# Moving seven weight conversions of an eight-core decoder block to earlier steps

## The chip, the cores and the metric

The kernel runs on all 8 cores of one Trainium2 chip. Each core works on two of the 16 sequences; the cores do not exchange data. The metric is the device time of the slowest core, in microseconds (us), and fast executions are compared with fast executions. A program on all cores has a second, slower state in which the cores of one die, rarely of both, get a lower clock (one run of after took 2790 us, with a mean clock of 0.861 on one die and 0.997 on the other).

For effects of a few us I also use a quieter number, called the **core mean** here: the mean span of the four cores of a die, averaged over all dies of a kernel's timed runs whose four cores all had a granted clock above 0.99. It keeps the undisturbed die of a slow run and does not hang on the one slowest core. Its scatter from die to die is about 2 us; 8 to 21 dies stand behind each value for an experiment and its reference, so the difference of two core means is uncertain by about 0.5 to 1 us (1.6 for the noisiest kernel).

## The reference, cut to what matters

```python
def swiglu(h, w_gate, w_up, w_down):
    return (jax.nn.silu(h @ w_gate) * (h @ w_up)) @ w_down

x = x + 0.5 * swiglu(rmsnorm(x, ffn1_norm), ffn1_w_gate, ffn1_w_up, ffn1_w_down)   # FFN 1
h = rmsnorm(x, mix_norm) @ w_in                    # pool values | q | k | v | forget logits
...                                                # pooling mixer | forgetting attention, 8 heads
x = x + concat([y_pool, y_attn]) @ w_out
x = x + 0.5 * swiglu(rmsnorm(x, ffn2_norm), ffn2_w_gate, ffn2_w_up, ffn2_w_down)   # FFN 2
```

All weights are float32 inputs. x is 16 x 2048 x 1024; the FFN width is 2816, which is 22 blocks of 128.

## The kernel before

**Units and conversions.** The FFN work of a core is cut into eight units of 1024 tokens; a unit has 22 gate/up steps and 8 down steps (steps 22 to 29). Unit 3 is the first that uses FFN 2. Its gate and up weights are converted once from float32 to bf16, from DRAM to DRAM, by 22 DMAs issued from POOL (the GpSimd engine); each is released when the FFN reaches a given step of a given unit. Weights are then loaded through small rings: ring A (gate/up, three buffers), ring B (down, four halves) and ring M (mixer, two buffers). Attention and the mixer are interleaved with the FFN.

```python
UNITS = [(0, 0), (0, 1), (0, 2), (1, 0), (0, 3), (1, 1), (1, 2), (1, 3)]   # (FFN, group of tokens)
# ...
def converts():
    # ...
    jobs += [(2 + i // 18, i % 18, wgu[1][i], wgu_s[1][i], [("wgu", 1, i)]) for i in range(NFF)]
    jobs += [(3, 5 + 2 * i, wd[1][i], wd_s[1][i], both(1, i)) for i in range(NKC)]
    for n, (u, fl, src, dst, keys) in enumerate(jobs):
        tr.add_dma_sem(f"cv{n}")
        yield ev_step[(u, fl)]                      # wait until the FFN reaches step fl of unit u
        yield Op("pool", [], keys, lambda e, src=src, dst=dst: e.dma_start(out=dst, in_=src),
                 c_dma(128 * src.shape[-1] * 4), sem=f"cv{n}")
```

**A scheduler in the host program.** Streams (FFN, attention, loads, conversions, ...) yield operations with modelled costs. At build time the scheduler takes, again and again, the operation that its model says can begin first. So the order of instructions on every engine is fixed at build time, and it depends on the modelled time of every DMA, at an assumed rate of `DMA_GB = 285.0`.

```python
def emit(self, op):
    # ...
    if op.sem is not None:                                          # a DMA
        self.tr.dma(op.eng, op.sem, op.reads, op.writes, op.emit)
        self.free[op.eng] = t + (1000.0 if op.eng == "pool" else 60.0)
        other = self.dma_free["sp" if op.eng == "pool" else "pool"]
        begin = max(self.dma_free[op.eng], t + 1300.0)
        end = begin + op.cost                                       # later DMAs queue up behind it
        # ...
```

## Time and profile before

| | before |
|---|---|
| median of 40 runs | 2447.49 us (2444.03 to 2881.26; those over about 2481 are slow-state runs) |
| cores of the profiled run | 2437.7 to 2445.4 us, clock 0.996 to 0.998 |
| busy on the slowest core | TensorE 98%, VectorE 67%, ScalarE 59%, POOL 23% |

The page of the slowest core: the span, engine busy times with their shares, and the start of the chain of work that ended last, by engine.

```profile
span 2445.4 us, 39669 instructions; the slowest of 8 cores (2437.7 to 2445.4 us)
...
PE 2386.1 (98%) x11862; PEld 1074.2 (44%) x12094; DVE 1638.8 (67%) x2424; ACT 1440.4 (59%) x2857; POOL 569.7 (23%) x793
...
PE 87%; DMA 5%; ACT 3%; issue 3%; DVE 2%; SPq 0%; ACTq 0%; DVEq 0%; POOLq 0%; POOL 0%
```

TensorE is the bound. The Trainium skill, "Perfetto Trace Analysis", section "Identifying the Most-Contended Engine", warns that matmul busy share does not measure the distance to peak, because pipelined matmuls look smaller in a trace. So I use the 98% only to say where to look for lost time: in TensorE's idle gaps and in the stretches at a lower clock. Core 1 serves for the readings below. The timeline at the start of unit 2 (start and duration of the issue, engine, line, what is moved):

```profile
587.72 0.54 POOL L525 DMA_DIRECT2D wgu2s<-wgu  x1
...
588.31 3.00 SPq L576 DMA_DIRECT2D sb_xsF<-yT  x3
...
589.66 1.08 POOL L525 DMA_DIRECT2D wgu2s<-wgu  x2
...
592.93 0.54 SPq L576 DMA_DIRECT2D sb_xsF<-yT  x1
```

and the summary of those four loads of the mixer's input (`xsF`) in 585 to 612 us:

```profile
DMA to landing us min/median/max: 15.0/22.3/33.2
```

Three conversions and four 512 KB loads are issued within about 5 us, and the last load takes 33.2 us to land; the median of such loads over the whole run is 8.5 us on this core (8.0 on the slowest core's page). The windows of core 1 (stretch, busy time and count of each engine, granted clock, DMA share, GB/s):

```profile
core 1: us, PE busy (x) PEld busy (x) DVE busy (x) ACT busy (x) POOL busy (x), PEclk, DMA share, GB/s
540.00:590.00 50.00, 50.00 (x240) 22.29 (x238) 20.01 (x27) 2.69 (x8) 8.92 (x16) 1.00 0.83 261
590.00:640.00 50.00, 47.69 (x245) 19.37 (x244) 43.12 (x57) 43.05 (x95) 19.80 (x25) 0.97 0.90 181
...
1160.00:1180.00 20.00, 20.00 (x134) 11.57 (x132) 17.95 (x35) 6.30 (x16) 3.20 (x7) 1.00 0.75 237
```

TensorE is full at the end of unit 1 (540 to 590), loses 2.3 us at the start of unit 2, and the mean clock of 0.97 there is one stretch of 3.4 us at half clock, near 617. TensorE's waits on core 1 from 500 to 1200 us (who waited for whom: total us, times, longest):

```profile
PE ps L847 <- DMA sb_wA<-wgu1s: 2.3, 1, 2.3
PE ps L847 <- DVE sb_sg L305: 1.9, 3, 0.8
PE ps L1075 <- ACT sb_PT L1179: 1.3, 3, 0.7
...
PE ps L874 <- DVE sb_sg L305: 0.7, 1, 0.7
```

Line 847 is the gate/up matmul, 874 the down matmul, 897 the mixer's projections.

### The profile page before, as it was taken

How to read it: one execution, taken by the hardware profiler on the slowest of the kernel's cores; microseconds unless marked ns; L12 is line 12 of the kernel's file. 1: busy time of each engine (PE TensorE's matmuls, PEld its weight loads, DVE VectorE, ACT ScalarE, POOL GpSimd, SP SyncE). 2: the span in 40 equal slices, each digit the busy share in tenths (PEclk: the TensorE clock that was granted, in tenths of full speed). 3: DMA queues.
4: the chain of work that ended last, by engine and by line, in shares of the span. 5: the costliest groups of instructions: out<-in, count | busy, mean ns of one | idle time of the engine just before them, and what ended most of it. 6: DMA issues, size and time to landing. Idle time of an engine off the chain costs nothing.

```text
span 2445.4 us, 39669 instructions; the slowest of 8 cores (2437.7 to 2445.4 us)
## 1 busy us (share of the span) xinstructions
PE 2386.1 (98%) x11862; PEld 1074.2 (44%) x12094; DVE 1638.8 (67%) x2424; ACT 1440.4 (59%) x2857; POOL 569.7 (23%) x793
## 2 busy tenths in 40 slices
PE   8999999999899999999999999999999999999998
PEld 4444444444444444443445444453434434444444
DVE  5763658656886977598756687268696799634541
ACT  4652457743686747688535875169674799514540
POOL 0114213332331332213332113223133101110000
PEclk9999999999999999999999999999999999999999
DMA  7999777588747456763564334642544621463225
GB/s 180 189 215 223 174 192 160 122 222 217 184 131 190 154 163 168 194 164 89 186 209 168 120 122 131 209 134 84 194 139 149 198 94 61 140 207 112 77 75 151
DMA packets 126530, 384.61 MB, mean 157 GB/s; under 512 B 15088, under 2 KB 15216, under 8 KB 126320
## 3 DMA queue, kind: packets, MB, share of 16 engines
q0 software_dynamic: 57200, 215.25, 35.7%
q1 hardware_dynamic: 69120, 166.81, 20.6%
q8 instruction: 102, 1.67, 0.3%
q14 instruction: 108, 0.88, 0.1%
HBM read 362.73 MB, written 91.24 MB: 186 GB/s over the span
## 4 chain that ended last, share of the span: by engine, by line
PE 87%; DMA 5%; ACT 3%; issue 3%; DVE 2%; SPq 0%; ACTq 0%; DVEq 0%; POOLq 0%; POOL 0%
PE ps L847 42%; PE ps L874 25%; PE ps L897 11%; PE ps L1075 3%; PE ps L1331 2%; PE ps L1116 2%; ACT sb_PT L1179 2%; DMA sb_wA<-wgu 1%; DMA sb_xsF<-yT 1%; PE ps L588 1%; DMA sb_wM<-wins 1%; PE ps L912 1%; PE ps L1159 0%; DMA sb_xsF<-xT 0%; DMA wgu1s<-sb_wA 0%
## 5 line engine op out<-in xcount | busy, mean ns | idle before, releaser
L847 PE MATMUL ps<-sb_hF,sb_wA 128*128 128x512 bf16 x5501 | 1254.4, 380 | 26.6 <-DVE sb_sg L305 6.1
L847 PEld LDWEIGHTS ps<-sb_hF,sb_wA 128*128 128x128 bf16 x5632 | 538.7, 98 | 698.8 <-issue 79.2
L874 PE MATMUL ps<-sb_act,sb_wB 128*128 128x512 bf16 x2753 | 623.0, 379 | 6.9 <-issue 2.5
L1179 ACT ACTIVATE sb_PT<-ps,sb_BT 128x256 bf16<-128x256 f32 (+1 forms) x1152 | 433.5, 491 | 118.3 <-PE ps L1075 59.7
L770 ACT ACTIVATE sb_sg<-sb_sg 128x512 f32<-128x512 f32 x352 | 227.5, 646 | 416.8 <-DVE sb_sg L767 395.2
L874 PEld LDWEIGHTS ps<-sb_act,sb_wB 128*128 128x128 bf16 x2816 | 272.0, 98 | 338.7 <-issue 18.7
L767 DVE TENSOR_TENSOR sb_sg<-sb_sg,ps 128x512 f32<-128x512 f32 x352 | 240.6, 684 | 159.1 <-PE ps L847 149.5
L783 DVE TENSOR_TENSOR sb_act<-sb_sg 128x512 bf16<-128x512 f32 x352 | 275.2, 782 | 70.3 <-ACT sb_sg L775 67.5
L1206 DVE TENSOR_TENSOR sb_acc<-sb_acc,sb_PT 128x1024 f32<-128x1024 f32 (+3 forms) x264 | 298.6, 1131 | 23.4 <-ACT sb_PT L1179 11.5
L772 ACT ACTIVATE sb_sg<-sb_sg,sb_cst 128x512 f32<-128x512 f32 x352 | 259.6, 737 | 20.6 <-ACT sb_sg L770 1.5
L815 DVE SCALAR_TENSOR_TENSOR sb_xr<-ps,sb_xr 128x512 f32<-128x512 f32 x128 | 88.0, 688 | 254.2 <-PE ps L874 237.3
L775 ACT ACTIVATE sb_sg<-sb_sg 128x512 f32<-128x512 f32 x352 | 227.2, 645 | 19.7 <-ACT sb_sg L772 0.7
L305 DVE COPY sb_sg<-ps 128x512 f32<-128x512 f32 x224 | 153.1, 683 | 47.2 <-PE ps L847 46.9
L897 PE MATMUL ps<-sb_hm,sb_wM 128*128 128x512 bf16 x755 | 176.7, 379 | 4.9 <-DMA sb_wM<-wins 4.0
L613 POOL TENSOR_TENSOR sb_na<-sb_na,sb_sq 128x512 f32<-128x512 f32 x120 | 149.6, 1247 | 66.0 <-ACT sb_sq L582 60.1
L582 ACT ACTIVATE sb_sq<-sb_xsF 128x512 bf16<-128x512 f32 x184 | 116.4, 655 | 66.4 <-DMA sb_xsF<-xT 27.1
L455 POOL DMA_DIRECT2D sb_wA<-wgu2s x88 | 47.9, 545 | 400.8 <-PE ps L847 327.9
L553 ACT ACTIVATE sb_rs<-ps,sb_cst 128x512 f32<-128x512 f32 x104 | 71.4, 691 | 86.4 <-PE ps L588 79.8
L897 PE MATMUL ps<-sb_yc,sb_wM 128*128 128x512 bf16 x499 | 119.8, 379 | 0.9 <-DVE sb_yc L1407 0.2
L1187 POOL TENSOR_SCALAR_AFFINE_SELECT sb_PT<-sb_PT 128x256 bf16<-128x256 bf16 x128 | 77.0, 605 | 176.1 <-ACT sb_PT L1179 175.4
L897 PEld LDWEIGHTS ps<-sb_hm,sb_wM 128*128 128x128 bf16 x768 | 74.7, 98 | 94.7 <-issue 6.3
L1271 DVE TENSOR_TENSOR sb_xsF<-ps,sb_xsF 128x512 f32<-128x512 f32 x64 | 44.2, 691 | 75.7 <-PE ps L897 75.7
(104 smaller groups left out, 1703.3 us busy)
## 6 DMA issues: line engine op xcount, KB each, us to landing
sb_xsF<-yT SPq DMA_DIRECT2D x96, 512.0 KB, 8.0
sb_wA<-wgu2s POOLq DMA_DIRECT2D x88, 512.0 KB, 3.8
sb_wA<-wgu1s POOLq DMA_DIRECT2D x66, 512.0 KB, 5.4
yT<-sb_xr SPq DMA_DIRECT2D x128, 256.0 KB, 4.2
sb_wM<-wins POOLq DMA_DIRECT2D x44, 512.0 KB, 3.9
sb_wB<-wd2s POOLq DMA_DIRECT2D x64, 352.0 KB, 4.4
sb_wB<-wd1s POOLq DMA_DIRECT2D x48, 352.0 KB, 4.7
sb_xr<-xT SPq DMA_DIRECT2D x64, 256.0 KB, 4.5
```

The costliest lines, as they stand in the source:

```text
L305: return Op("dve", reads, writes, lambda e: e.tensor_copy(out=out, in_=in_), c_dve(n), alt=Op("act", reads, writes, lambda e: e.copy(out=o ...
L613: lambda e, a_=a_, sl=sl: e.tensor_tensor(out=na[:], in0=a_, in1=sq_t[:, tok(sl)], op=ALU.add), c_pool(TT))
L767: lambda e: e.tensor_tensor(out=gu, in0=g, in1=ps[bu][:], op=ALU.mult), c_dve(TT))
L770: lambda e: e.activation(out=g, in_=g, func=AF.Exp, scale=-1.0), c_act(TT, False))
L772: lambda e: e.activation(out=g, in_=g, func=AF.Ln, bias=one_t, scale=1.0),
L775: lambda e: e.activation(out=g, in_=g, func=AF.Exp, scale=-1.0), c_act(TT, False))
L783: lambda e: e.tensor_tensor(out=act_ap(fl, t2), in0=g, in1=gu, op=ALU.mult),
L847: ins = e.matmul(ps[b][:], lhsT=w[:, part * 1024 + kc * 128: part * 1024 + (kc + 1) * 128], rhs=hF[:, kc * 1024 + t2 * TT: kc * 1024 + (t2 ...
L874: ins = e.matmul(ps[b][:], lhsT=w[:, k:k + 128], rhs=act_ap(fl, t2), start=(fl == 0), stop=(fl == NFF - 1))
L897: ins = e.matmul(ps[bank][:], lhsT=w[:, off + kc * 128: off + (kc + 1) * 128], rhs=src[:, tok(kc)], start=(kc == 0), stop=(kc == NKC - 1))
L1179: lambda e, s_=s_, a=a, z=z, hq=hq, b=b, pt=pt, c=c, j=j: e.activation(out=PT[:, pt * 1024 + s_ * TT + a: pt * 1024 + s_ * TT + z], in_=ps ...
L1206: lambda e, w=w, a_=a_: e.tensor_tensor(out=a_, in0=a_, in1=w, op=ALU.add),
```

## The change

The aim is to break up the burst: conversions 0 to 2 go to the last three down steps of unit 1, and 18 to 21 from the start of unit 3 to unit 2's last four gate/up steps (18 to 21; its down steps follow). Conversions 3 to 17 keep their steps. No operation is added or removed.

```diff
-            jobs += [(2 + i // 18, i % 18, wgu[1][i], wgu_s[1][i], [("wgu", 1, i)]) for i in range(NFF)]
+            jobs += [(1 if i < 3 else 2, i + 27 * (i < 3), wgu[1][i], wgu_s[1][i], [("wgu", 1, i)]) for i in range(NFF)]
```

## The prediction

> **What bounds the kernel.** TensorE. The page has PE busy 2386.1 of 2445.4 us (98%), and the chain that ended last is 87% PE, 5% DMA. The list of cores gives 2437.7 to 2445.4 us at clocks of 0.996 to 0.998. On the slowest core (6) the groups of waits hold about 43 us of PE idle, most of it in stages that the change does not touch; one wait on a ring A load, 1.5 us, lies in unit 2.
>
> **What the change does.** No operation is added or removed: the same 22 DRAM-to-DRAM conversions (1 MB read, 512 KB written each), issued from POOL. Conversions 0 to 2 move from the start of unit 2 to the last down steps of unit 1; 18 to 21 move from the start of unit 3 to the end of unit 2.
>
> **What that touches.**
> 1. Start of unit 2. The timeline shows three conversions issued at 587.5 to 589.9 us (FFN steps 0 to 2 open together) just as four loads of the mixer's input are issued at 588.1 to 592.5. The last lands 35.7 us after its issue; the median is 8.0. Windows 600-620 and 620-640 have a DMA share of 1.00 and 0.74, and PE busy only 18.1 and 16.9 of 20. The waits in 587-660 are about 6.5 us (attention's exponentials, ring A, VectorE; about 2 to 5 on most other cores). Cores 1, 4 and 6 also show one clock dip to 0.5 for 3.4 us near 617 to 630, worth about 1.7 us. The Trainium skill, "TensorE: Matmul & The Clock Gate", section "What's actually happening", says that an idle window of about 3.4 us halves the clock; the dip's length agrees. Without the burst I expect the last load 15 to 20 us earlier, and 2 to 4 us of idle and dip gone on the slowest cores.
> 2. Start of unit 3 (933-977): four conversions leave; input loads there take 11 to 16 us, and PE waits about 2 us in 923-1020. Gain 0 to 1 us. The end of unit 2 (800-823), where they go, has a DMA share of 0.30.
> 3. Cost: about 550 to 587 us already has a DMA share of 0.80 or more. A conversion takes 5 to 7 us alone, 10 to 24 in a crowd. The Trainium skill, "DMA: Bandwidth & Descriptors", section "Issuing engines are not separate DMA queues", says that all issuers interleave on the same 16 engines; the trace agrees, SyncE's loads slow beside POOL's conversions. So down weights (5 to 6 us to land, four half buffers of about 6 us work each), mixer weights (two buffers) and residual loads get slower. The buffers cover most of it: 0 to 2 us of new PE waits, and the third conversion may still overlap the mixer's input loads.
>
> Net: about -2 us on the slowest core, 0.1%. The instruction order comes from a scheduler that models DMA time, so later parts may be reordered; I guess +/-4 us for that.
>
> **Prediction.** 2445 us, range 2438 to 2454. Faster by over 2%: 0.01; within 2%: 0.98; slower: 0.01.
>
> **What would show it.** The input loads at unit 2's start landing in 15 to 20 us; DMA share in 550-587 near 1.0 and lower in 590-640; PE waits in 590-660 down to 1 to 3 us; the dip near 620 gone on most cores; conversions ending before unit 3; PE busy unchanged.
>
> **What would make it wrong.** Waits on ring B or the mixer's weights in 550-590 long enough to cool the clock; a reordered attention; a median holding slow-state runs (2489.9 and 2668.9 before look like such).

## More of the kernel before

**PSUM banks.** PSUM is the memory that this kernel's matmuls write their sums to. Attention and the FFN share one pool of eight of its banks, so what holds a bank decides when the next FFN pair may begin. In the first tile of a sequence, attention's sums are divided straight from PSUM (lines 1229 to 1249):

```python
def att_short(t, c, X, Y, pairs):
    # ...
    for q in range(4):
        qs = slice(q * 128, (q + 1) * 128)
        yield Op("dve", [("ps", Y)], [("rs", r)],
                 lambda e, qs=qs: e.reciprocal(out=rc[:, qs], in_=ps[Y][:, qs]), 861.0)   # L1237
    MB.put(Y)                                       # only now is bank Y free
```

## The result, and the profile after

| | before | after |
|---|---|---|
| median | 2447.49 us (40 runs) | 2451.93 us (20 runs) |
| ratio of fast runs, 95% interval | | 1.0022 (1.0012 to 1.0031) |
| cores of the profiled run | 2437.7 to 2445.4 us | 2442.7 to 2451.8 us |
| their mean | 2441.5 us | 2446.8 us (+5.3) |

A ratio is the mean time of one kernel's fast runs over that of the other's of the same rounds, so it is not quite the ratio of the medians. The change costs 0.2%: clear of noise, and far inside the 2% that would count as slower. The page:

```profile
span 2451.8 us, 39635 instructions; the slowest of 8 cores (2442.7 to 2451.8 us)
...
PE 2394.3 (98%) x11861; PEld 1076.4 (44%) x12094; DVE 1631.9 (67%) x2424; ACT 1435.8 (59%) x2857; POOL 572.2 (23%) x793
```

What the change was made for did happen. The timeline of core 1 from 550 to 594 (conversion 0 is issued before it, at 536.5), and the landing times of the same four loads:

```profile
551.80 0.54 POOL L525 DMA_DIRECT2D wgu2s<-wgu  x1
...
567.84 0.53 POOL L525 DMA_DIRECT2D wgu2s<-wgu  x1
...
585.47 1.40 SPq L576 DMA_DIRECT2D sb_xsF<-yT  x3
...
591.35 0.56 SPq L576 DMA_DIRECT2D sb_xsF<-yT  x1
```

```profile
DMA to landing us min/median/max: 8.6/9.6/10.6
```

The windows of core 1:

```profile
core 1: us, PE busy (x) PEld busy (x) DVE busy (x) ACT busy (x) POOL busy (x), PEclk, DMA share, GB/s
540.00:590.00 50.00, 49.29 (x237) 21.52 (x234) 23.23 (x32) 4.99 (x13) 8.64 (x15) 1.00 0.95 245
590.00:640.00 50.00, 48.16 (x254) 20.06 (x253) 46.94 (x63) 46.16 (x102) 23.98 (x28) 1.00 0.69 172
...
1160.00:1180.00 20.00, 16.77 (x79) 6.23 (x78) 14.02 (x22) 12.35 (x28) 12.99 (x15) 0.83 0.22 76
```

The start of unit 2 is better (DMA share 0.69 instead of 0.90, full clock), the end of unit 1 a little worse. The large loss is in the third row, half a millisecond later, where no conversion runs at all and the DMA queues are nearly idle (0.22). The waits of core 1 from 500 to 1200:

```profile
PE ps L847 <- DVE sb_rs L1237: 2.9, 1, 2.9
PE ps L847 <- DVE sb_sg L305: 2.4, 6, 0.7
PE ps L847 <- ACT sb_sg L306: 1.2, 1, 1.2
PE ps L1159 <- ACT sb_sg L306: 1.2, 1, 1.2
...
PE ps L897 <- DMA sb_wM<-wouts: 0.7, 1, 0.7
...
```

The wait on L1237 is new. It is 2.9 us on every one of the 8 cores, and on none before. The timeline shows it as it happens; in brackets stands the idle time before an instruction and what ended it:

```profile
1164.71 0.96 DVE L1237 RECIPROCAL sb_rs<-ps 128x128 f32<-128x128 f32 x1
...
1164.89 1.89 PE L847 MATMUL ps<-sb_hF,sb_wA 128*128 128x512 bf16 x8 [0.29 <-DVE sb_sg L767]
1165.59 0.63 DVE L1019 SCALAR_TENSOR_TENSOR sb_xm<-sb_xm 128x512 f32<-128x512 f32 x1
1166.13 1.75 DVE L1237 RECIPROCAL sb_rs<-ps 128x128 f32<-128x128 f32 x2
...
1167.81 0.89 DVE L1024 TENSOR_TENSOR sb_fix<-sb_xm,sb_invc 128x7 f32<-128x7 f32 x1
1168.62 0.94 DVE L1237 RECIPROCAL sb_rs<-ps 128x128 f32<-128x128 f32 x1
...
1169.72 1.86 PE L847 MATMUL ps<-sb_hF,sb_wA 128*128 128x512 bf16 x4 [2.94 <-DVE sb_rs L1237]
```

The next FFN pair needs the bank that holds attention's sums. VectorE frees it after four reciprocals of about 0.95 us, with work of the pooling mixer (L1019, L1024) between them. Six of the 8 cores then run 3.4 or 6.8 us at half clock, beginning between 1169 and 1181 (from the clock records of the trace; core 1's window above shows it as 0.83). In before's order the same reciprocals run between 1224 and 1237, and TensorE does not wait for them. The Trainium skill, "TensorE: Matmul & The Clock Gate", section "What's actually happening", says that the clock is halved after an idle window of about 3.4 us and that the window runs freely. That the same wait on all 8 cores halves the clock on only six fits a freely running window; that a wait of 2.9 us is enough does not fit a window that is idle throughout (see the last section).

**Is the work in the same order?** No. Compared instruction by instruction, TensorE's orders are the same for the first 3086 weight loads (to about 625 us) and again for the last 4350 (from about 1545 us), and differ between. The orders of the other engines part a little earlier: SyncE's transfers at about 553 us, ScalarE and VectorE at about 600. The scheduler had seen other DMA times. From the times at which the 8 cores reach TensorE's two points, after stands on average -0.6 us against before at the first, +4.8 at the second and +5.3 at the end (these are two single executions; between the two points single cores lost 0.7 to 10.8 us). The loss lies where the order differs.

The next table sums, per core, TensorE's idle gaps of over 150 ns, and adds the time lost to a lower clock (length of a stretch times one minus its clock); means of 8 cores, us. Other kernels' rows are explained below.

| stretch, us | 500-600 | 600-700 | 700-800 | 800-900 | 900-1000 | 1000-1100 | 1100-1200 | sum |
|---|---|---|---|---|---|---|---|---|
| before | 0.0 | 3.6 | 2.5 | 0.4 | 1.6 | 0.4 | 1.0 | 9.5 |
| after | 0.9 | 2.1 | 1.2 | 2.2 | 1.0 | 1.8 | 5.7 | 14.9 |
| before's order, after's conversions | 1.7 | 1.8 | 2.5 | 0.4 | 1.5 | 0.6 | 1.0 | 9.5 |
| after's order, before's conversions | 0.0 | 6.1 | 1.9 | 2.2 | 1.3 | 1.8 | 4.7 | 18.0 |

The sums of the first two rows differ by 5.4 us, the spans by 5.3.

### The profile page after: what moved, and what is told of

It reads as the page before. It is cut to its first block, busy times and chain, and to the rows that moved or that the text cites. A ratio compares the mean times of both kernels' runs of the same rounds, so it can differ in the third digit from the quotient of the medians.

```text
span 2451.8 us, 39635 instructions; the slowest of 8 cores (2442.7 to 2451.8 us)
## 1 busy us (share of the span) xinstructions
PE 2394.3 (98%) x11861; PEld 1076.4 (44%) x12094; DVE 1631.9 (67%) x2424; ACT 1435.8 (59%) x2857; POOL 572.2 (23%) x793
## 4 chain that ended last, share of the span: by engine, by line
PE 88%; issue 3%; ACT 3%; DVE 3%; DMA 2%; POOL 0%; SPq 0%; DVEq 0%; ACTq 0%; POOLq 0%
PE ps L847 44%; PE ps L874 24%; PE ps L897 11%; PE ps L1075 3%; PE ps L1331 2%; PE ps L1116 2%; ACT sb_PT L1179 2%; PE ps L588 1%; PE ps L912 1%; ACT sb_sg L772 1%; DMA sb_xsF<-xT 1%; DMA sb_wM<-wins 0%; DMA sb_wM<-wouts 0%; PE ps L1159 0%; DVE sb_sg L305 0%
## 5 line engine op out<-in xcount | busy, mean ns | idle before, releaser
L783 DVE TENSOR_TENSOR sb_act<-sb_sg 128x512 bf16<-128x512 f32 x352 | 268.6, 763 | 57.3 <-ACT sb_sg L775 56.6
L455 POOL DMA_DIRECT2D sb_wB<-wd2s x64 | 34.8, 543 | 246.6 <-PE ps L874 228.0
```

The costliest lines, as they stand in the source:

```text
L783: lambda e: e.tensor_tensor(out=act_ap(fl, t2), in0=g, in1=gu, op=ALU.mult),
```

## The experiments

**Theory R (reordering):** moving the conversions is nearly neutral in itself; the loss is made by the instruction order that the scheduler came to because its modelled DMA times changed. **Theory C (contention), the rival:** the moved DMA traffic itself slows what runs beside it, at the end of unit 1 or of unit 2.

The edits below are shortened; `...` marks cuts. To tell them apart I separated plan and issue: the scheduler goes on planning with one set of steps, while the real conversions are issued at the other set and are invisible to the plan. The orders on TensorE, VectorE, ScalarE and SyncE were compared with those of the kernel named and are the same; only the conversions' places in POOL's queue differ. All kernels gave correct results. The first four ran on one chip, the second four on another, the last four on a third, each group beside its own runs of before (core means 2440.0, 2440.1 and 2442.9 us). After itself, in its own 20 timed runs and profiled ones, has a core mean of 2446.4; a comparison with it may hold a difference between chips.

| kernel | ratio (95%) | core mean, against before on the same chip |
|---|---|---|
| before's order, after's conversions | 1.0000 (0.9983 to 1.0016) | 2439.5, -0.5 |
| after's order, before's conversions | 1.0034 (1.0021 to 1.0048) | 2448.3, +8.3 |
| only conversions 0 to 2 moved | 1.0064 (1.0009 to 1.0119) | 2446.4, +6.4 |
| only conversions 18 to 21 moved | 1.0038 (0.9993 to 1.0083) | 2441.2, +1.2 |
| after, bank copied out first, 8 places | 1.0015 (1.0000 to 1.0030) | 2444.5, +4.4 |
| before, bank copied out first, 8 places | 1.0021 (1.0003 to 1.0039) | 2444.1, +4.0 |
| before's order, conversions late | 1.0001 (0.9988 to 1.0014) | 2438.7, -1.4 |
| before, assumed DMA rate 288 | 1.0014 (1.0002 to 1.0027) | 2442.6, +2.5 |
| after, bank copied out once | 0.9987 (0.9949 to 1.0026) | 2444.8, +1.9 |
| before, bank copied out once | 0.9986 (0.9948 to 1.0024) | 2442.4, -0.5 |
| before's order, conversions in unit 2's down steps | 1.0015 (0.9942 to 1.0088) | 2445.8, +2.9 |
| before, assumed DMA rate 284 | 1.0001 (0.9958 to 1.0044) | 2446.9, +4.0 |

On the third chip two of before's runs, of 2459 and 2475 us with one pair of cores slower, still counted as fast; they pull the ratios of the last four rows down and widen them. There the core mean is the better guide.

### Plan and issue apart: the two crossed kernels

```diff
-            jobs += [(2 + i // 18, i % 18, wgu[1][i], ...
+            jobs += [(*((1 if i < 3 else 2, i + 27 * (i < 3)) if issue else (2 + i // 18, i % 18)), wgu[1][i], ...
+                # (in words) plan stream (issue=False): a wgu conversion only advances the scheduler's model
+                # (in words) issue stream (issue=True): the real DMA; the model does not see it
```

The second kernel has the two sets of steps swapped.

> The instruction order of the kernel before on TensorE, VectorE, ScalarE and SyncE (compared, the same), with the 22 conversions issued where the change puts them. Theory R (the loss is made by the new instruction order in units 2 to 4): ratio to before 0.997 to 1.000, all orders' new waits (2.9 us on the reciprocal near 1170, the clock dip there, about 2 us in 800-900) absent, input loads at the start of unit 2 land in 6 to 12 us as after. Theory C (the moved DMA traffic itself costs the time): ratio 1.0015 to 1.003, as the change.

> The instruction order of the kernel after, with the conversions issued at the steps of before. Theory R: ratio to before 1.002 to 1.004 (the new waits stay, and the burst at the start of unit 2 comes back on top, loads there 15 to 36 us). Theory C: ratio 0.999 to 1.001.

With before's order and after's conversions the loss is gone: ratio 1.0000, core mean -0.5. With after's order and before's conversions it is all there and more: 1.0034, +8.3. On core 1 of the first, the only wait of TensorE from 1100 to 1200 us is

```profile
PE ps L874 <- DVE sb_sg L305: 0.7, 1, 0.7
```

and on core 1 of the second, with no conversion moved:

```profile
PE ps L847 <- DVE sb_rs L1237: 2.9, 1, 2.9
...
```

The loads of the mixer's input follow the conversions and not the order: on core 1 they land quickly in the first kernel and slowly in the second.

```profile
DMA to landing us min/median/max: 5.6/6.7/8.8
```

```profile
DMA to landing us min/median/max: 12.1/20.3/28.0
```

Theory R holds; theory C can not explain either result. But C is not empty. At a fixed order the table of losses shows what the move itself does: 600-700 falls from 3.6 to 1.8, and 500-600 rises from 0.0 to 1.7. The gain at the start of unit 2 is paid for at the end of unit 1. Core 5 of the first kernel shows the bill from 540 to 600, and the clock in its window:

```profile
PE ps L897 <- DMA sb_wM<-wouts: 3.0, 1, 3.0
```

```profile
560.00:580.00 20.00, 16.96 (x72) 7.22 (x71) 3.46 (x5) 0.00 (x0) 2.12 (x4) 0.91 0.97 242
```

The mixer's weights, with only two buffers, come late while the DMA engines are 97% busy: the load issued at 561.2 us took 13.7 us to land, and 8.0 us in before, where it was issued at 561.1. Then the clock halves for 3.4 us. The Trainium skill, "DMA: Bandwidth & Descriptors", section "Issuing engines are not separate DMA queues", says that all issuers' transfers interleave on the same 16 engines. The trace agrees at the start of unit 2, where SyncE's loads on core 1 took up to 33.2 us beside POOL's conversions and up to 8.8 us without them, at the same order. At the end of unit 1 the late weights are issued by POOL too, so this trace does not separate sharing of the engines from waiting behind the conversions in POOL's own queue.

### One part of the change alone

```diff
-(2 + i // 18, i % 18, ...)
+(1, i + 27, ...) if i < 3 else (2 + i // 18, i % 18, ...)      # only 0 to 2
+(2, i, ...)                                                    # only 18 to 21
```

> Only conversions 0 to 2 move (to the last down steps of unit 1); 18 to 21 stay at the start of unit 3. Its order on TensorE, VectorE and ScalarE is the same as after the change. Theory R: ratio 1.0015 to 1.003, as the change. Theory C: if the cost is in unit 1's down steps the same 1.0015 to 1.003; if it is in the end of unit 2, about 1.000.

> Only conversions 18 to 21 move (to the end of unit 2); 0 to 2 stay at the start of unit 2. Its order is nearly that of before (31 lines of TensorE's differ, near the start of unit 3). Theory R: ratio 0.999 to 1.0005, no stall near 1170. Theory C with the cost in the end of unit 2: 1.0015 to 1.003 with PE waits in 800-900 as after.

Moving the first three alone gives after's order on every engine but POOL, and after's loss: core mean +6.4, the stall on L1237, a half-clock stretch there on 6 of 8 cores. Moving the last four alone leaves the order nearly as before and the core mean within 1.2 us. Both ratios are blurred: each has a run of about 2476 to 2482 us among its fast ones, and only four fast runs. The ratio of 1.0038 of the second is over what theory R expected, but its interval holds 1.000; I go by its core mean, which is within about twice its uncertainty of zero. Its profile, cores 0 to 3: no wait on L1237.

### The stall at L1237 taken away

If bank Y is copied to SBUF first, it is free after one copy of 0.69 us and the reciprocals are taken from the copy. The scheduler's plan is kept, so the order of all other instructions is unchanged (the cut shows the version for all eight places; `recip(e, a, z)` takes reciprocals a to z - 1).

```diff
-            for q in range(4):
-                yield Op("dve", [("ps", Y)], [("rs", r)], lambda e: e.reciprocal(out=rc[:, qs], in_=ps[Y][:, qs]), 861.0)
+            # four planned operations as before: the copy; reciprocals 0 and 1; 2; 3 - the last three read only rs
+            for q, emit in enumerate([lambda e: e.tensor_copy(out=rc, in_=ps[Y][:]), lambda e: recip(e, 0, 2),
+                                      lambda e: recip(e, 2, 3), lambda e: recip(e, 3, 4)]):
```

> After, with one thing changed: in the short attention tiles VectorE copies the sum bank to SBUF first (one copy, about 0.7 us) and takes the reciprocals from the copy, so that the bank comes free after the copy and not after four reciprocals of 0.95 us. Order and conversions are those of after on TensorE, ScalarE, POOL and SyncE. If the stall near 1170 (2.9 us on the reciprocal) and the half-clock stretch behind it (1.7 us where it falls) are a main part of the loss: that stall under 0.7 us, no dip at 1165-1185, and the mean of the cores of undisturbed dies 3 to 4.5 us below that of after (2446.4), ratio to before 1.0003 to 1.001. If that stall is covered elsewhere: ratio stays 1.002.

> Control: the same copy in the kernel before, whose order has no wait on that reciprocal. Ratio 0.9995 to 1.0005, mean of cores within 1 us of before. If it gains 3 us or more here too, the copy helps in a way that has nothing to do with the new order.

The stall and the half-clock stretch went away on all 8 cores, yet the core mean fell by 1.9 us only, not by 3 to 4.5 (2446.4 to 2444.5), and the ratio of 1.0015 is over the 1.0003 to 1.001 expected: a miss. And the control was not neutral, as I had expected: 4.0 us slower than before. The eight extra copies cost time elsewhere: TensorE's idle time rises by 1.2 to 1.4 us at 400 to 500, and in the control again by 1.5 us at 1300 to 1400 (this is read from cores 4 to 7 of both kernels). So this experiment mixes two things, and its number for the stall can not be used. The next pair makes the copy in one place only, `(t, c) == (4, 0)`, which is the stalled one.

> As after_copy_first, but the copy only in the one tile whose reciprocals held the bank (first pair of the second sequence's first tile); the other seven keep their reciprocals from PSUM. If the stall near 1170 and its half-clock stretch are the main part of what the new order costs: mean of cores 3 to 4.5 us below after (2446.4), that is 2442 to 2443.5, and no dip at 1165-1185. If the 1.4 us on ScalarE that took the stall's place before, and other waits, matter more: 2444 to 2446.

> Control of after_copy_once: the same single copy in the order of before. Mean of cores within 1 us of before, since the seven other copies, which cost about 4 us in before_copy_first, are gone.

Now the control is neutral (-0.5). After with the single copy is +1.9 against before on its chip. My expectation missed: 2444.8 lies in the range that I had given for "other waits matter more". But it had named absolute times of another chip, and this chip's before was 2.8 us slower, so I compare with +5.3 (after's profile) or +6.4 (only the first three moved, the same order). By that the stall and its clock penalty were 3.4 to 4.5 us of the loss, uncertain by about 1 us. The trace of this kernel, which needs no comparison of chips, agrees: its losses at 1100 to 1200 are 2.5 us, against 5.7 in after and 1.0 in before, so 3.2 us came back. No core has a dip between 1165 and 1185. The window of core 1 there (0.83 was its clock in after):

```profile
1160.00:1180.00 20.00, 17.60 (x99) 7.29 (x98) 17.31 (x33) 15.92 (x37) 11.18 (x14) 1.00 0.25 79
```
And its waits from 1100 to 1200:

```profile
PE ps L1075 <- ACT sb_PT L1179: 1.7, 1, 1.7
...
```

A smaller wait, on attention's exponentials, takes the stall's place, and the other new waits of that order (800-900 and 1000-1100 in the table of losses) stay, at 2.2 and 1.9 us. The remaining loss of 1.9 us was not taken apart by an experiment; these waits are where I would look.

### Other draws of the same lottery

If any small change of modelled DMA times can reorder the program, it should need no conversion at all.

```diff
-DMA_GB = 285.0
+DMA_GB = 288.0      # and, in another kernel, 284.0
```

> The kernel before, conversions untouched, with only the scheduler's assumed DMA rate changed from 285 to 288: it reorders TensorE rows 255 to 447 of 1266 and nothing in the work. If any reordering of this kind costs or gives some us by chance (theory R's root): ratio anywhere in 0.998 to 1.004, clear of 1.000 by more than 1 us in the mean of cores. If the order of before is not special and reorderings are neutral: within 1 us.

> The kernel before with the scheduler's assumed DMA rate changed from 285 to 284: TensorE rows 183 to 295 of 1266 reordered, conversions at their old steps. A second draw of the same lottery as before_gb288 (which was 2.5 us slower in the mean of cores): anything from -2 to +6 us; only the spread matters. Within 1 us would say that most reorderings are neutral.

A change of 1% or less in an assumption of the host program, with the same work and the same conversion steps, gave +2.5 us (288; TensorE's order parts after 3026 weight loads and is the same again for the last 6042 of 12094, about 614 to 1210 us in before) and +4.0 us (284; 2396 and 8392, about 485 to 749 us). The losses of their profiles in 500 to 1200, counted as in the table above, are 12.4 and 12.7 us against before's 9.5, and they rise where the order differs. Rates of 286 and 287 leave TensorE's order as it is; these were only compared and not run. So a reordering without any moved conversion costs some us, if less than the change's +5 to +6. The three larger reorderings that I measured all lost time. That fits a program whose order was kept because it was good, but three draws do not prove it.

### Looking for a version that beats both

At the order of before, the conversions can be put anywhere. First three steps later, with the last three in unit 2's down steps; then with the last seven there.

```diff
+2, 3 + i if i < 19 else 22 + 2 * (i - 19)      # issue steps of the first
+2, 3 + i if i < 15 else 7 + i                  # issue steps of the second
```

> Order of before on TensorE, VectorE, ScalarE and SyncE; conversion i issued at step 3 + i of unit 2, and the last three in unit 2's down steps (DMA share there about 0.3 to 0.5): neither the burst at the start of unit 2 nor extra load on unit 1's last down steps. Waits in 600-640 about 1 to 2 us lower as with the change's placement, none new in 500-600 (which had about 1.4 us on average there and a dip on two cores). Mean of cores 1 to 3 us below before, ratio 0.9985 to 1.000. If conversions at unit 1's end cost nothing in truth, it is the same as with the change's placement (-0.5 us).

> Order of before; conversions 0 to 14 at steps 3 to 17 of unit 2 (three steps later than in before), 15 to 21 in the first seven down steps of unit 2. No burst at unit 2's start, nothing added to unit 1, nothing at 760-800 where order_before_conv_late waited 2 us on the mixer's weights. Mean of cores 2 to 3.5 us below before, ratio 0.9985 to 0.9997; no dip near 617 or 780. If the traffic finds a new place to cost as much (down weights or mixer weights in 823-943): within 1 us.

The first is the best kernel by core mean, -1.4 us, but its time is that of before (ratio 1.0001); I do not call it faster. Four of its cores wait near 780 us for the mixer's weights, as here on core 1:

```profile
PE ps L897 <- DMA sb_wM<-wouts: 2.3, 1, 2.3
...
```

The second was meant to avoid that place and failed: +2.9 us. Core 1 waits there still, and longer, and then in the down steps, where I had seen room (DMA share of before about 0.5 at 823 to 943):

```profile
PE ps L897 <- DMA sb_wM<-wouts: 4.3, 1, 4.3
PE ps L588 <- DVE sb_xr L815: 2.1, 1, 2.1
...
```

The wait near 780 is not explained by the conversions that I moved away from there; its chip was also the noisiest of the three (the dies of this kernel scatter by 4.3 us, so +2.9 is less than twice its uncertainty), and I leave its size open. What stands is that no placement tried gained more than the noise.

## Why the prediction was right or wrong

- **Right: the time within 2% and inside the range** (2438 to 2454; measured 2451.93), and TensorE as the bound. But the forecast was 2 us less, and the change costs about 5 us more. That it fell inside the range is owed to the width allowed for reordering, not to a foreseen mechanism; in part it is luck.
- **Right: the burst and its removal.** On core 6, the core that the prediction read, the four input loads took 7.1 us at most, the last one 5.9 instead of 35.7 (15 to 20 were expected, so the relief was larger). The DMA share of 540-590 on core 1 is 0.95, and 0.69 after it. The half-clock stretch near 620 is gone from all cores. Core 6's waits in 587-660 fell to 2.3 us. The last conversion is issued at 803 us on core 1, well before unit 3 (about 943).
- **Mis-sized: the net of the move itself.** The prediction put 2 to 4 us gained against 0 to 2 us of new waits. At fixed order, the losses show 1.8 us gained at 600-700 and 1.7 us paid at 500-600; the core mean moved by -0.5 us (uncertain by 0.75), where the prediction had -2. The mechanism of the cost was named rightly (the mixer's two buffers).
- **Wrong: the sign of the total, through one term.** The step that failed is "The instruction order comes from a scheduler that models DMA time, so later parts may be reordered; I guess +/-4 us for that", with zero in its middle. The reordering cost 6.9 us (only the first three moved, which has after's order, less before's order with after's conversions: 2446.4 - 2439.5; the last four conversions sit differently in these two) or 8.3 us (with before's conversions). It was the largest term of all. It came from a stretch from 625 to 1545 us, most of which lies after the last moved conversion (803 us on core 1).
- **What the reordering did, as shown:** one PSUM bank held 2.9 us too long by reciprocals that now fell just before an FFN pair, with half clock behind it on 6 of 8 cores. Its removal gave back 3.2 us in the trace and 3.4 to 4.5 by core means. The rest of the reordering's cost is located (800-900, 1000-1100) but not shown by an experiment.
- **Where the conversions may help more:** with after's order, moving the first three from before's steps saves 1.9 us (2448.3 to 2446.4, on one chip), against 0.5 for all seven with before's order. The difference is within about twice its uncertainty; the losses of single profiles point the same way (18.0 to after's 14.9, against 9.5 to 9.5). That the gain from a burst taken away depends on what stands next to it is a reading of this, not shown.

## What to carry to other kernels

When a build-time scheduler orders the instructions, a change of *when a transfer is issued* is two changes: the transfer moves, and the program is reordered. Keep the plan fixed and move only the issue to see the first alone; perturb an unrelated constant of the model to see how large the second can be. Compare the instruction orders before explaining a difference of a few tenths of a per cent, and find the points where they part and meet again: if the time is lost between these points and far from the moved work, the order is the suspect.

## What the Trainium skill lacked or had wrong

- "TensorE: Matmul & The Clock Gate", section "Seeing it yourself": it says to budget 13/16 of the clock for sustained dense matmul on all cores. Here all eight cores ran dense matmuls for 2.4 ms at a mean granted clock of 0.995 to 0.998 in the fast state. A clock of 0.812 appeared for 3.7 to 5.9 us at a time in the fast profiles of before and after; it lasted only in the two slow runs that were profiled, for 535 to 1638 us, and there on one die (mean clock 0.885 to 0.886 and 0.948 to 0.958).
- The same page, section "What's actually happening": it gives an idle window of about 3.4 us as what halves the clock. Longest listed waits of 2.9 us (1170, six of 8 cores), 3.0 us (core 5 of the first crossed kernel) and even 2.3 us (core 1 of before, near 617) were followed by a half-clock stretch. In the last 3.4 us before each half-clock stretch between 400 and 2400 us in before, after and the first crossed kernel, TensorE was still busy for 0.5 to 1.4 us, so a window need not be idle throughout. Ends of matmuls are modelled in the trace, so idle times are not exact.
- "DMA: Bandwidth & Descriptors" gives no time for a DRAM-to-DRAM transfer that converts float32 to bf16. Here one of 1 MB read and 512 KB written took 5 to 7 us to land in quiet stretches and up to 24.8 us in the burst (core 4 of before).
- No page that I read has the price of holding a PSUM bank for a reciprocal: 0.95 us for 128 x 128 float32 on VectorE, against 0.69 us for a copy of the whole 128 x 512 bank.
